# Block transposes by four SBUF-to-SBUF copies, in a two-layer decoder trunk on one Trainium2 core

## The chip, the core and the metric

The kernel runs on one NeuronCore of a Trainium2 chip: TensorE (PE, with its weight loads PEld), VectorE (DVE), ScalarE (ACT), GpSimd (POOL) and SyncE (SP), each with its own instruction queue, and 16 DMA engines that all queues share. SBUF and PSUM are on the core, HBM outside it. The metric is the device time of one execution in microseconds. Before the change it is 1225.33 us, the median of three runs (1224.45 to 1226.32).

## The reference

Two layers; each is a half-step feed-forward, a mixer of three branches, and a second half-step feed-forward. x is 256 tokens by 1024 channels, all in float32.

```python
for l in range(DEPTH):                                   # DEPTH = 2
    h = rms_norm(x, ffn1_norm_pre[l])
    x = x + 0.5 * rms_norm(swiglu(h, ffn1_w_in[l], ffn1_w_out[l]), ffn1_norm_post[l])
    h = rms_norm(x, mix_norm_pre[l])
    y = token_mixer(h, mem, cos, sin, mem_norm[l], w_mix_in[l], ...)
    x = x + rms_norm(y, mix_norm_post[l])
    h = rms_norm(x, ffn2_norm_pre[l])
    x = x + 0.5 * rms_norm(swiglu(h, ffn2_w_in[l], ffn2_w_out[l]), ffn2_norm_post[l])

# swiglu: a, b = split(h @ w_in); (silu(a) * b) @ w_out          D_FF = 2816
# token_mixer: one projection of h gives everything; then
#   short convolution; sparse attention (compressed, selected, window), 8 heads of 64;
#   cross-attention into 256 memory tokens, 4 heads of 128, keys and values = rms_norm(mem) @ w_mem_kv
#   merged = sum of sigmoid(gate_i) * (branch_i @ w_branch_i);  merged @ w_mix_out
```

## The kernel before

**Tiling.** The 256 tokens are two tiles of 128, called t = 0 and t = 1. Each is a stream (L1340) that runs through both layers; the two streams share each weight unit, and stream 0 may lead by up to three steps (LEAD). A step is six matmuls of 128x512 or as much. Every weight unit of 128x1024 words is loaded by SP into a buffer "raw" (four of them), and then split into a rounded part and a rest, "whi" by ACT (L309) and "wlo" by DVE (L310); each product is three matmuls (hi·hi, hi·lo, lo·hi). So ACT and DVE spend most of their time on these splits, which run ahead of TensorE as far as eight pairs of buffers let them.

**The order.** The program is written out step by step. `advance` (L349) counts steps; `later(n, fn)` puts work n steps on; `background` (L1231) lets the memory, compression and attention tasks each take a turn beside the streams. `prefetch` (L316) issues loads and splits some steps ahead of use. SP keeps the order as written; the order of the other engines is decided when the program is built. Each engine then runs its queue in that order, and an instruction that waits holds up everything behind it.

**The turn.** Activations have to change places: a tile with tokens on the partitions becomes one with channels on them. For the wide ones `turn` (L419) does this in two parts. DVE transposes 32x32 blocks inside the tile into "blocks" (L423). Then the 32x32 blocks themselves have to move between partition groups: one step later (AWAY) GpSimd issues four DMAs that write them to a scratch "there" in HBM (L428), and four steps after the start (BACK) one DMA that loads the scratch as "moved" (L440). That load waits on GpSimd for the landing of the four, and later DMAs queue behind it. At a fixed number of steps after the start, `turn_beside` (L448) splits "moved" into "turnhi" (ACT, L452) and "turnlo" (DVE, L453), which TensorE reads. The number is SPLIT = 12 in the feed-forward, ATT_T = 10 in attention, and KEYS = 18 for the memory's keys. There are 42 such turns: 24 in the feed-forwards (three per stream and feed-forward, the third 768 wide), 16 in attention and two for the memory's keys; the two of the memory in layer 0 come beside them.

**The memory.** `memory` (L688) normalizes the 256 memory tokens in two halves. In layer 0 each half is turned by way of its own scratch "mthere", with SPLIT steps to wait, and then scaled ("mf", L694). In layer 1 the halves are loaded again from mthere (RETURN = 6 steps). Then come two rounds of products with w_mem_kv, whose loads SP interleaves with the stream's own.

**Weights.** A turned tile has its rows in an order that the weights' rows have to match. For the five matrices in TURNED (L62) each unit is loaded by two DMAs, one for each half of the rows, to every second partition (L292).

**Prenorm.** At each sub-layer `postnorm` squares y on ACT ("junk", L463), updates x on DVE (L539); TensorE transposes x, and `prenorm` (L475) makes "hThi" on ACT (L491). TensorE cannot begin the next product before that.

Of the kernel before, what the change touches and what calls it, by code (L numbers as in the profile page):

```python
# [44 lines left out]
WARM = 5, 1, 2  # L45
KEYS, HALF, SECOND = 18, 5, 2
FRONT = True
# [6 lines left out]
NORM_B, NORM_C = 1, 1  # L54
AWAY, BACK, SPLIT, RETURN = 1, 4, 12, 6
DBUFS = 8
CONV, BS, CMP, ZC, QS_0, QS_1, QM, PC, YM = 4, 4, 6, 2, 2, 6, 2, 3, 1
ATT_A, ATT_B, ATT_C, ATT_D, ATT_T = 1, 3, 2, 6, 10
EARLY, RAMP, SCALES, STAGED, SETUP = 6, 10, 5, 8, 30
PACE, PACE_1, PACED = 9, 8, ("nsa", "memory")  # L60

TURNED = ("ffn1_w_out", "ffn2_w_out", "w_mix_out", "w_branch_conv", "w_branch_mem")  # L62
PRE = ("ffn1_norm_pre", "mix_norm_pre", "ffn2_norm_pre", "mem_norm")
# [59 lines left out]


def f32(ap):
    return ap.bitcast(F32)


def trunk_kernel(tc: tile.TileContext, a, out: bass.AP):
    with ExitStack() as ctx:  # L130
        def pool(name, bufs, **kw):
            return ctx.enter_context(tc.tile_pool(name=name, bufs=bufs, **kw))

        pools = dict(
            consts=pool("consts", 1), rawp=pool("rawp", RAWBUFS), wp=pool("wp", WBUFS), gp=pool("gp", GBUFS),
            gbp=pool("gbp", GAINS), tp=pool("tp", TBUFS), sp_pool=pool("sp", 2),
            dram=pool("dram", DBUFS, space=bass.MemoryType.DRAM),
            psa=pool("psa", ABUFS, space=bass.MemoryType.PSUM),
            pst=pool("pst", 8 - ABUFS, space=bass.MemoryType.PSUM))
        nothing = Nothing()  # L140
        plan = program(nothing, nothing, {k: nothing for k in pools}, nothing, nothing, None)
        with tc.manual_schedule(engines={mybir.EngineType.SP}):
            program(tc, tc.nc, pools, a, out, plan)


def program(tc, nc, pools, a, out, plan):
# [115 lines left out]
    def load(item, engines=None):  # L262
# [10 lines left out]
        for off, step, name, l, k0, nk, c0, n in parts:  # L273
# [144 lines left out]

    def turn(src, n, finish, wait, there=None):  # L419
        f = n // 4  # L420
        make = gtile if n > 512 else ttile
        blocks = make("blocks")
        nc.vector.transpose(blocks[:, :n], view(src, 0, [[32, 4], [P, n // P], [1, 32]]))  # L423
        there = dram.tile([P, 1024], F32, name="there", tag="d") if there is None else there

        def away():
            for q in range(4):
                nc.gpsimd.dma_start(there[:, q * f:(q + 1) * f].rearrange("(p j) f -> j p f", j=32),  # L428
                                    blocks[q * 32:(q + 1) * 32, :n].rearrange("j (p f) -> j p f", p=4))

        later(AWAY, away)
        back(there, n, finish, BACK, wait)

    def back(there, n, finish, start, wait):
        make = gtile if n > 512 else ttile
        moved = []

        def go():
            moved.append(make("moved"))
            nc.gpsimd.dma_start(moved[0][:, :n], there[:, :n])  # L440

        later(start, go)
        later(wait, lambda: finish(view(moved[0], 0, [[32, n // P], [n // 4, 4], [1, 32]])))

# [241 lines left out]
    mthere = [dram.tile([P, 1024], F32, name=f"mthere{i}", tag=f"m{i}", bufs=1) for i in range(2)]  # L686

    def memory(l):  # L688
        S = shared[l]
        H = []  # L690
        for mt in range(2):
# [9 lines left out]
            if l == 0:  # L701
# [3 lines left out]
                norm_scales(m, 0, mscale[mt])  # L705
                turn(m, 1024, gained, SPLIT, mthere[mt])
                yield SPLIT
            else:
                back(mthere[mt], 1024, gained, 0, RETURN)
                yield RETURN  # L710
# [12 lines left out]
        for mt in range(2):  # L723
            nc.scalar.activation(view(ks, mt * P, [[256, 4], [1, P]]), ps[mt].rearrange("p (h m) -> p h m", h=4),
                                 AF.Copy, scale=H[mt][1][0])

# [121 lines left out]

    def softmax_part(s3, dg, sums, place):
        n = s3.shape[1] if not dry else 1  # L850
# [3 lines left out]
        for i in range(n):  # L854
            dst, k = place(i)
            nc.scalar.activation(dst, s3[:, i], AF.Exp, bias=nm[:, i:i + 1], accum_out=sums[:, k:k + 1])

# [54 lines left out]
    def nsa_first(l, g):  # L912
# [4 lines left out]
        for u in range(2):  # L917
# [9 lines left out]
            def place(c):  # L927
                k = c % 2 * 4 + u * 2 + c // 2
                return p[:, k * P:(k + 1) * P], k

            s4 = s.rearrange("p (c k) -> p c k", c=4)
            softmax_part(s4, s4, sums, place)
        yield ATT_B
# [7 lines left out]
    def nsa_second(l, var, g):  # L941
# [5 lines left out]
        for u in range(2):  # L947
            s = bank("s")
            s3 = s.rearrange("p (i k) -> p i k", i=2)
            for i in range(2):  # L950
                for j in range(2):
# [3 lines left out]
            softmax_part(s3, s3[:, :, P:2 * P], sums,  # L955
                         lambda i: (view(p, (u * 2 + i) * P, [[512, 2], [1, P]]), u * 2 + i))
        yield ATT_B
# [159 lines left out]
    def mem_attention(l, u):  # L1117
# [5 lines left out]
        for t in range(2):  # L1123
# [11 lines left out]
            for i in range(2):  # L1135
                k = i * 2 + t
                nc.scalar.activation(view(p, k * P, [[512, 2], [1, P]]), s3[:, i], AF.Exp, bias=nm[:, i:i + 1],
                                     scale=scale, accum_out=sums[:, k:k + 1])
# [274 lines left out]
```

## Time and profile before

| | |
|---|---|
| median of three runs | 1225.33 us |
| profiled execution | 1228.28 us |
| its span, first to last instruction | 1226.6 us |
| mean granted TensorE clock | 0.994 |
| DMA packets | 281.63 MB, 230 GB/s in the mean |
| HBM read, written | 257.44 MB, 23.07 MB |
| longest shares of the chain that ended last | PE 70%, DMA 11%, DVE 8%, ACT 5% |

The profile is of one execution. Its tables count for each engine how long it was busy and, for each stretch of idle time, which event ended it. A row of a timeline has the start and the length in us, the engine, the line, what is written from what, and in brackets the idle time before it and what ended that. "PEclk" or the granted clock is the share of TensorE's full rate that it was given. A busy TensorE counts as busy at a low clock too, so both have to be read.

### The profile page before, as it was taken

Reading aid. Unit: us, or ns where it says so; the run is one execution under the profiler, and the core shown is the slowest. Engines: PE = TensorE matmul, PEld = TensorE weight load, DVE = VectorE, ACT = ScalarE, POOL = GpSimd, SP = SyncE. Lnnn points to the kernel's source line nnn. Section 1 sums busy time; section 2 is a strip of 40 time slices with the busy share of each in tenths; the row PEclk is TensorE's granted clock in tenths of the full one; section 3 lists DMA queues with packets and bytes.
Section 4 is the critical chain, followed back from the end, with each engine's and each line's share of the span. In section 5 each row is a group of like instructions: output and inputs, shape, how many; then the busy total and the mean of one; then the engine's idle time right before and its main releaser. Section 6 shows DMA issues by size and latency. Waiting matters only on the chain.

```text
span 1226.6 us, 16793 instructions
## 1 busy us (share of the span) xinstructions
PE 1192.9 (97%) x5776; PEld 1035.9 (84%) x5776; DVE 904.0 (74%) x1157; ACT 721.5 (59%) x1139; POOL 193.0 (16%) x383
## 2 busy tenths in 40 slices
PE   8999998999999999999999999999999989999997
PEld 6888877888888888888878888888878878888886
DVE  7867567798998776676576776578899866767753
ACT  6655345887876564554454554569878645645542
POOL 5011311311121010111011011013022200110110
PEclk9999998999999999999999999999999999999999
DMA  7888857677588757787757788858668866677772
GB/s 259 274 252 269 285 180 253 204 247 217 179 267 257 227 167 228 257 277 227 229 183 229 255 257 268 259 155 246 208 189 249 261 215 204 184 231 253 257 243 83
DMA packets 134293, 281.63 MB, mean 230 GB/s; under 512 B 13536, under 2 KB 32640, under 8 KB 134208
## 3 DMA queue, kind: packets, MB, share of 16 engines
q1 hardware_dynamic: 118752, 234.59, 60.9%
q0 software_dynamic: 15136, 45.44, 11.6%
q8 instruction: 45, 0.74, 0.2%
q10 hardware_dynamic: 320, 0.53, 0.1%
q14 instruction: 40, 0.33, 0.1%
HBM read 257.44 MB, written 23.07 MB: 229 GB/s over the span
## 4 chain that ended last, share of the span: by engine, by line
PE 70%; DMA 11%; DVE 8%; ACT 5%; issue 4%; POOL 2%; DVEq 0%; POOLq 0%; SPq 0%; ACTq 0%
PE acc L382 32%; PE acc L372 5%; PE acc L370 5%; PE acc L371 5%; PE y L372 5%; PE y L371 5%; PE y L370 5%; DMA moved<-there 3%; DVE wlo L310 3%; DMA there<-blocks 3%; DMA moved<-mthere 1%; ACT whi L309 1%; PE pt L413 1%; PE br L370 1%; PE br L372 1%
## 5 line engine op out<-in xcount | busy, mean ns | idle before, releaser
L310 DVE TENSOR_TENSOR wlo<-raw,whi 128x1024 fp32r<-128x1024 f32 (+2 forms) x441 | 530.8, 1212 | 185.6 <-ACT whi L309 181.7
L309 ACT CAST whi<-raw 128x1024 fp32r<-128x1024 f32 (+2 forms) x441 | 453.1, 1038 | 299.6 <-PE acc L382 155.1
L382 PE MATMUL acc<-whi,hThi 128*128 128x512 f32 x640 | 191.9, 381 | 3.2 <-ACT hThi L491 2.6
L382 PE MATMUL acc<-wlo,hThi 128*128 128x512 f32 x640 | 191.9, 380 | 0.1
L382 PE MATMUL acc<-whi,hTlo 128*128 128x512 f32 x640 | 191.6, 381 | 0.1
L370 PE MATMUL acc<-whi,hThi 128*128 128x512 f32 (+1 forms) x480 | 184.3, 384 | 3.6 <-ACT hThi L491 3.6
L371 PE MATMUL acc<-wlo,hThi 128*128 128x512 f32 (+1 forms) x480 | 180.5, 376 | 0.0
L372 PE MATMUL acc<-whi,hTlo 128*128 128x512 f32 (+1 forms) x480 | 180.1, 375 | 0.1
L428 POOL DMA_DIRECT2D there<-blocks x168 | 92.2, 555 | 451.0 <-DVE blocks L423 365.4
L382 PEld LDWEIGHTS acc<-whi,hThi 128*128 128x128 f32 x640 | 120.7, 189 | 21.6 <-ACT hThi L491 3.7
L382 PEld LDWEIGHTS acc<-whi,hTlo 128*128 128x128 f32 x640 | 121.1, 190 | 18.5 <-DVE hTlo L492 1.4
L382 PEld LDWEIGHTS acc<-wlo,hThi 128*128 128x128 f32 x640 | 121.3, 190 | 17.7 <-DVE wlo L310 0.5
L371 PE MATMUL y<-wlo,turnhi 128*128 128x512 f32 x352 | 133.4, 380 | 2.4 <-DVE wlo L310 2.4
L372 PE MATMUL y<-whi,turnlo 128*128 128x512 f32 x352 | 133.2, 379 | 0.0
L370 PE MATMUL y<-whi,turnhi 128*128 128x512 f32 x352 | 132.6, 379 | 0.0
L370 PEld LDWEIGHTS acc<-whi,hThi 128*128 128x128 f32 x480 | 91.4, 191 | 15.5 <-ACT hThi L491 4.8
L372 PEld LDWEIGHTS acc<-whi,hTlo 128*128 128x128 f32 x480 | 91.4, 190 | 12.6 <-DVE hTlo L492 0.3
L371 PEld LDWEIGHTS acc<-wlo,hThi 128*128 128x128 f32 x480 | 91.6, 191 | 10.3
L453 DVE TENSOR_TENSOR turnlo<-moved,turnhi 128x1024 fp32r<-128x1024 f32 (+1 forms) x42 | 49.2, 1170 | 54.1 <-ACT turnhi L452 54.0
L452 ACT CAST turnhi<-moved 128x1024 fp32r<-128x1024 f32 (+1 forms) x42 | 42.1, 1002 | 63.0 <-DMA moved<-there 54.9
L371 PEld LDWEIGHTS y<-wlo,turnhi 128*128 128x128 f32 x352 | 66.5, 189 | 12.1 <-DVE wlo L310 2.8
L370 PEld LDWEIGHTS y<-whi,turnhi 128*128 128x128 f32 x352 | 66.5, 189 | 9.4
(302 smaller groups left out, 1458.6 us busy)
## 6 DMA issues: line engine op xcount, KB each, us to landing
raw<-in_ffn_w_in_dram SPq DMA_DIRECT2D x159, 512.0 KB, 4.9
raw<-in_w_mix_in_dram SPq DMA_DIRECT2D x96, 512.0 KB, 4.8
raw<-in_ffn_w_out_dram SPq DMA_DIRECT2D x176, 256.0 KB, 4.3
there<-blocks POOLq DMA_DIRECT2D x136, 128.0 KB, 4.5
moved<-there POOLq DMA_DIRECT2D x34, 512.0 KB, 5.2
raw<-in_ffn_w_in_dram SPq DMA_DIRECT2D x33, 256.0 KB, 4.1
raw<-in_w_mem_kv_dram SPq DMA_DIRECT2D x16, 512.0 KB, 6.1
raw<-in_w_mix_out_dram SPq DMA_DIRECT2D x32, 256.0 KB, 3.5
```

The lines of the kernel that those rows point to most:

```text
L309: pinned(nc.scalar.copy(hi[:, c0:c1], raw[:, c0:c1]))
L310: pinned(nc.vector.tensor_sub(lo[:, c0:c1], raw[:, c0:c1], f32(hi[:, c0:c1])))
L370: nc.tensor.matmul(ps, lhsT=xh, rhs=wh, start=start, stop=False, skip_group_check=skip)
L371: nc.tensor.matmul(ps, lhsT=xh, rhs=wl, start=False, stop=False, skip_group_check=skip)
L372: nc.tensor.matmul(ps, lhsT=xl, rhs=wh, start=False, stop=stop, skip_group_check=skip)
L382: pinned(nc.tensor.matmul(p[:, :n], lhsT=hT[x2][:, k], rhs=moving(w, j * n, n), start=(k == 0 and i == 0), stop=(k == 7 and i == 2)))
L413: pinned(nc.tensor.transpose(pt[:, j * P:(j + 1) * P], src[:, c0 + j * P:c0 + (j + 1) * P], ident))
L428: nc.gpsimd.dma_start(there[:, q * f:(q + 1) * f].rearrange("(p j) f -> j p f", j=32), blocks[q * 32:(q + 1) * 32, :n].rearrange("j (p f) ...
L452: nc.scalar.copy(hv, mv)
L453: nc.vector.tensor_sub(lv, mv, f32(hv))
```

## The change

The scratch in HBM goes. The four DMAs write straight into "moved" in SBUF, one step after the transpose, and the load back is gone. Because the four DMAs now place partition 4j + p where the load had placed 32p + j, the order of what is turned changes with them:

- Softmax results are written in the new order: the Exp on ACT reads PSUM at a stride of four words and writes runs of 32 (`lanes_in`, `lanes_out`). The keys are copied in the same way.
- The weight rows follow: TURNED becomes RUNS, with runs of 16 rows for both w_out and of 64 for the other three matrices, and the unit is loaded by one DMA per 128 rows instead of two of 64 partitions.
- The memory's halves are copied to mthere after their use, for layer 1.
- The steps to wait fall: SPLIT 12 to 8, ATT_T 10 to 7, KEYS 18 to 13; BACK and the eight scratch buffers go.

```diff
-KEYS, HALF, SECOND = 18, 5, 2
+KEYS, HALF, SECOND = 13, 5, 2
-AWAY, BACK, SPLIT, RETURN = 1, 4, 12, 6
-DBUFS = 8
+AWAY, SPLIT, RETURN = 1, 8, 6
-ATT_A, ATT_B, ATT_C, ATT_D, ATT_T = 1, 3, 2, 6, 10
+ATT_A, ATT_B, ATT_C, ATT_D, ATT_T = 1, 3, 2, 6, 7
-TURNED = ("ffn1_w_out", "ffn2_w_out", "w_mix_out", "w_branch_conv", "w_branch_mem")
+RUNS = {"ffn1_w_out": 16, "ffn2_w_out": 16, "w_mix_out": 64, "w_branch_conv": 64, "w_branch_mem": 64}
+def lanes_in(ap, c, n=P):
+    return view(ap, c, [[P, n // P], [1, 4], [4, 32]])
+def lanes_out(ap, c, dims):
+    return view(ap, c, [list(d) for d in dims] + [[32, 4], [1, 32]])
...
-                if name in TURNED:
-                    for h in range(2):
-                        rows = src.rearrange("(k h i) n -> h i k n", h=2, i=64)[h]
-                        nc.sync.dma_start(view(raw[h:P:2], off, [[step, nk], [1, n]]), rows)
+                if name in RUNS:
+                    rows = src.rearrange("(k v u) n -> k u v n", k=nk, u=RUNS[name])
+                    for k in range(nk):
+                        nc.sync.dma_start(raw[:, off + k * step:off + k * step + n], rows[k])
...
-    def turn(src, n, finish, wait, there=None):
+    def turn(src, n, finish, wait, order=(32, 1)):
...
-        nc.vector.transpose(blocks[:, :n], view(src, 0, [[32, 4], [P, n // P], [1, 32]]))
-        there = dram.tile([P, 1024], F32, name="there", tag="d") if there is None else there
+        nc.vector.transpose(blocks[:, :n], view(src, 0, [[order[0], 4], [P, n // P], [order[1], 32]]))
+        moved = []
         def away():
+            moved.append(make("moved"))
             for q in range(4):
-                nc.gpsimd.dma_start(there[:, q * f:(q + 1) * f].rearrange("(p j) f -> j p f", j=32),
+                nc.gpsimd.dma_start(moved[0][:, q * f:(q + 1) * f],
                                     blocks[q * 32:(q + 1) * 32, :n].rearrange("j (p f) -> j p f", p=4))
         later(AWAY, away)
-        back(there, n, finish, BACK, wait)
-    def back(there, n, finish, start, wait):
...
-            nc.gpsimd.dma_start(moved[0][:, :n], there[:, :n])
-        later(start, go)
+        later(wait, lambda: finish(turned_view(moved[0], n)))
...
+    def keep(mt, gained):
+        def finish(mv):
+            gained(mv)
...
+            nc.gpsimd.dma_start(mthere[mt], whole)
+    def back(mt, gained):
+        moved = gtile("moved")
+        nc.gpsimd.dma_start(moved, mthere[mt])
+        later(RETURN, lambda: gained(turned_view(moved, 1024)))
...
-            nc.scalar.activation(dst, s3[:, i], AF.Exp, bias=nm[:, i:i + 1], accum_out=sums[:, k:k + 1])
+            nc.scalar.activation(dst, lanes_in(s3[:, i], 0, width), AF.Exp, bias=nm[:, i:i + 1],
+                                 accum_out=sums[:, k:k + 1])
```

The built order moves at places where the diff shows nothing. On ACT at the first mixer's prenorm of stream 0 in layer 0, up to the hThi that TensorE needs ("ks" are the memory's keys, "vm" its values; 560 wide splits are of the mixer's second group of columns), the rows before are

```order
L463 ACTIVATE junk,ss_1829<-y_1231 128x512
L463 ACTIVATE junk,ss_1829<-y_1232 128x512
L309 CAST whi<-raw 128x1024
L724 ACTIVATE ks<-acc,mscale_127 128x4x128
L309 CAST whi<-raw 128x1024
L724 ACTIVATE ks<-acc,mscale_128 128x4x128
L309 CAST whi<-raw 128x1024 x5
L491 CAST hThi<-hf 128x512 x2
```

and of the change

```order
L414 ACTIVATE vm<-acc,mscale_127 128x512
L414 ACTIVATE vm<-acc,mscale_128 128x512
L316 CAST whi<-raw 128x1024
L316 CAST whi<-raw 128x560
L464 ACTIVATE junk,ss_1859<-y_1218 128x512
L464 ACTIVATE junk,ss_1859<-y_1219 128x512
L464 ACTIVATE junk,ss_1900<-x_88 128x512
L492 CAST hThi<-hf 128x512 x2
```

Seven splits and both copies of the keys stood between junk and hThi; now they, and the values too, stand ahead of junk. On ACT at the boundary of layer 0 and layer 1, stream 0 again, the rows before are

```order
L309 CAST whi<-raw 128x1024 x13
L463 ACTIVATE junk,ss_5859<-y_5417 128x512
L309 CAST whi<-raw 128x1024
L463 ACTIVATE junk,ss_5859<-y_5418 128x512
L309 CAST whi<-raw 128x1024 x4
L491 CAST hThi<-hf 128x512 x2
```

and of the change

```order
L316 CAST whi<-raw 128x1024 x17
L464 ACTIVATE junk,ss_5766<-y_5345 128x512
L464 ACTIVATE junk,ss_5766<-y_5346 128x512
L464 ACTIVATE junk,ss_5807<-x_88 128x512
L492 CAST hThi<-hf 128x512 x2
```

The five splits between the first junk and hThi have moved ahead of junk. On DVE at the last attention turn of layer 1 ("p" are the probabilities, "yf" the sums over branches' heads, "gth" and "merged" the gated merge), from the transpose to its turnlo, the rows before are

```order
L423 STREAM_TRANSPOSE blocks<-p 128x1024
L893 TENSOR_TENSOR yf<-o,yf 64x512
L310 TENSOR_TENSOR wlo<-raw,whi 128x1024
L893 TENSOR_TENSOR yf<-o,yf 64x512
L453 TENSOR_TENSOR turnlo<-moved,turnhi 128x1024
L310 TENSOR_TENSOR wlo<-raw,whi 128x1024 x2
L1326 SCALAR_TENSOR_TENSOR gth<-gth,br 128x512
L1327 TENSOR_TENSOR merged_8715<-merged_8715,gth 128x512
L310 TENSOR_TENSOR wlo<-raw,whi 128x1024 x2
L453 TENSOR_TENSOR turnlo<-moved,turnhi 128x1024
```

where the first turnlo belongs to the turn before, and of the change

```order
L430 STREAM_TRANSPOSE blocks<-p 128x1024
L317 TENSOR_TENSOR wlo<-raw,whi 128x1024 x3
L1340 SCALAR_TENSOR_TENSOR gth<-gth,br 128x512
L454 TENSOR_TENSOR turnlo<-moved,turnhi 128x1024
```

turnlo stands three splits behind its blocks instead of five, and the previous turn's turnlo is already done.

More of the change, by code (lines that the diff above doesn't have):

```diff
@@ L136, in trunk_kernel @@
             gbp=pool("gbp", GAINS), tp=pool("tp", TBUFS), sp_pool=pool("sp", 2),
-            dram=pool("dram", DBUFS, space=bass.MemoryType.DRAM),
+            dram=pool("dram", 1, space=bass.MemoryType.DRAM),
             psa=pool("psa", ABUFS, space=bass.MemoryType.PSUM),
@@ L422, in turn, with turned_view @@
         blocks = make("blocks")
-        nc.vector.transpose(blocks[:, :n], view(src, 0, [[32, 4], [P, n // P], [1, 32]]))
-        there = dram.tile([P, 1024], F32, name="there", tag="d") if there is None else there
+        nc.vector.transpose(blocks[:, :n], view(src, 0, [[order[0], 4], [P, n // P], [order[1], 32]]))
+        moved = []
         def away():
+            moved.append(make("moved"))
             for q in range(4):
-                nc.gpsimd.dma_start(there[:, q * f:(q + 1) * f].rearrange("(p j) f -> j p f", j=32),
+                nc.gpsimd.dma_start(moved[0][:, q * f:(q + 1) * f],
                                     blocks[q * 32:(q + 1) * 32, :n].rearrange("j (p f) -> j p f", p=4))
         later(AWAY, away)
-        back(there, n, finish, BACK, wait)
-    def back(there, n, finish, start, wait):
[L435 to L440, printed above, removed]
-        later(start, go)
-        later(wait, lambda: finish(view(moved[0], 0, [[32, n // P], [n // 4, 4], [1, 32]])))
+        later(wait, lambda: finish(turned_view(moved[0], n)))
+        return moved
+    def turned_view(moved, n):
+        return view(moved, 0, [[32, n // P], [n // 4, 4], [1, 32]])
     def quarters(ap, c):
@@ L686, in program @@
     mthere = [dram.tile([P, 1024], F32, name=f"mthere{i}", tag=f"m{i}", bufs=1) for i in range(2)]
+    def keep(mt, gained):
+        def finish(mv):
+            gained(mv)
+            whole = bass.AP(tensor=mv.tensor, offset=mv.offset, ap=[list(mv.ap[0]), [1, 1024]]) if not dry else mv
+            nc.gpsimd.dma_start(mthere[mt], whole)
+        return finish
+    def back(mt, gained):
+        moved = gtile("moved")
+        nc.gpsimd.dma_start(moved, mthere[mt])
+        later(RETURN, lambda: gained(turned_view(moved, 1024)))
     def memory(l):
@@ L705, in memory @@
                 norm_scales(m, 0, mscale[mt])
-                turn(m, 1024, gained, SPLIT, mthere[mt])
+                turn(m, 1024, keep(mt, gained), SPLIT, (1, 4))
                 yield SPLIT
             else:
-                back(mthere[mt], 1024, gained, 0, RETURN)
+                back(mt, gained)
                 yield RETURN
@@ L723, in memory @@
         for mt in range(2):
-            nc.scalar.activation(view(ks, mt * P, [[256, 4], [1, P]]), ps[mt].rearrange("p (h m) -> p h m", h=4),
-                                 AF.Copy, scale=H[mt][1][0])
+            nc.scalar.activation(lanes_out(ks, mt * P, [[256, 4]]), lanes_in(ps[mt], 0, 512), AF.Copy,
+                                 scale=H[mt][1][0])
         def keys(hi, lo):
@@ L847, in recip_gate, with softmax_part @@
         return r
-    def softmax_part(s3, dg, sums, place):
+    def softmax_part(s3, dg, sums, place, width):
         n = s3.shape[1] if not dry else 1
@@ L928, in place @@
                 k = c % 2 * 4 + u * 2 + c // 2
-                return p[:, k * P:(k + 1) * P], k
+                return lanes_out(p, k * P, [[0, 1]]), k
             s4 = s.rearrange("p (c k) -> p c k", c=4)
-            softmax_part(s4, s4, sums, place)
+            softmax_part(s4, s4, sums, place, P)
         yield ATT_B
@@ L955, in nsa_second @@
             softmax_part(s3, s3[:, :, P:2 * P], sums,
-                         lambda i: (view(p, (u * 2 + i) * P, [[512, 2], [1, P]]), u * 2 + i))
+                         lambda i: (lanes_out(p, (u * 2 + i) * P, [[512, 2]]), u * 2 + i), 2 * P)
         yield ATT_B
@@ L1136, in mem_attention @@
                 k = i * 2 + t
-                nc.scalar.activation(view(p, k * P, [[512, 2], [1, P]]), s3[:, i], AF.Exp, bias=nm[:, i:i + 1],
+                nc.scalar.activation(lanes_out(p, k * P, [[512, 2]]), lanes_in(s3[:, i], 0, 2 * P), AF.Exp, bias=nm[:, i:i + 1],
                                      scale=scale, accum_out=sums[:, k:k + 1])
```

## The prediction

> **What bounds the kernel now.** I read the page first, then a table of stretches, then the waits, then the timeline around each place where TensorE stood. The page's first section gives the frame:
>
> ```profile
> PE 1192.9 (97%) x5776; PEld 1035.9 (84%) x5776; DVE 904.0 (74%) x1157; ACT 721.5 (59%) x1139; POOL 193.0 (16%) x383
> ```
>
> TensorE is busy 97% of a 1226.6 us span, and the change leaves all 5776 matmuls in place. So the time can only move in the 33.7 us in which TensorE stands, and in stretches where its granted clock is low. The table of stretches says where those are (columns: length, busy time of PE, PEld, DVE, ACT and POOL with their counts, granted clock, DMA share, GB/s):
>
> ```profile
> 20.00:130.00 110.00, 110.00 (x511) 95.77 (x511) 83.41 (x101) 61.59 (x68) 20.45 (x37) 1.00 0.84 270
> 130.00:180.00 50.00, 47.58 (x221) 41.20 (x220) 26.34 (x26) 20.62 (x27) 11.43 (x24) 1.00 0.66 223
> 180.00:225.00 45.00, 40.92 (x185) 34.70 (x184) 32.49 (x42) 26.06 (x45) 7.81 (x15) 0.92 0.72 227
> 250.00:320.00 70.00, 66.35 (x373) 58.10 (x372) 63.14 (x128) 56.91 (x122) 9.69 (x19) 1.00 0.67 207
> 390.00:410.00 20.00, 19.44 (x92) 16.23 (x91) 17.17 (x19) 11.86 (x14) 0.00 (x0) 1.00 0.72 223
> 410.00:600.00 190.00, 189.65 (x892) 165.42 (x891) 129.84 (x135) 96.72 (x114) 21.88 (x40) 1.00 0.74 233
> 600.00:630.00 30.00, 28.03 (x129) 23.72 (x128) 20.74 (x30) 16.49 (x29) 4.33 (x10) 0.94 0.51 155
> 740.00:770.00 30.00, 29.08 (x134) 24.84 (x133) 19.60 (x18) 14.57 (x15) 4.35 (x8) 1.00 0.80 257
> 800.00:830.00 30.00, 29.31 (x153) 25.09 (x152) 21.60 (x32) 19.89 (x45) 4.67 (x12) 1.00 0.52 148
> 850.00:920.00 70.00, 66.82 (x378) 58.38 (x377) 63.02 (x127) 57.08 (x123) 10.36 (x19) 1.00 0.66 206
> 955.00:975.00 20.00, 18.03 (x87) 15.39 (x86) 16.81 (x25) 13.85 (x27) 2.74 (x5) 1.00 0.76 243
> 995.00:1015.00 20.00, 16.34 (x68) 12.97 (x67) 15.95 (x18) 10.68 (x13) 0.00 (x0) 0.91 0.52 160
> ```
>
> A feed-forward stretch (20 to 130) is solid: 511 matmuls in 110 us, 0.215 us each, so one step of the program (six matmuls) is 1.3 us. For the others I count standing time (length minus PE busy) plus clock time (1 minus the granted clock, times the length): A 130–180: 2.4. B 180–225: 4.1 + 3.6 = 7.7. Early attention, 250–320 and 850–920: 3.65 + 3.2. I 390–410: 0.6. C 600–630: 2.0 + 1.8 = 3.8. G 740–770: 0.9. D 955–975: 2.0. E 995–1015: 3.7 + 1.8 = 5.5. That is 29.8 us, and it is the whole stake. The clock is low only in B, C and E, each time behind a stop of 1.9 to 3.3 us (rows below). [...]
>
> **The change part by part.** *The return trip.* A turn was four pieces to HBM, a wait, and one load back; now the four pieces land where they are read.
>
> ```profile
> raw<-in_ffn_w_in_dram SPq DMA_DIRECT2D x159, 512.0 KB, 4.9
> raw<-in_ffn_w_out_dram SPq DMA_DIRECT2D x176, 256.0 KB, 4.3
> there<-blocks POOLq DMA_DIRECT2D x136, 128.0 KB, 4.5
> moved<-there POOLq DMA_DIRECT2D x34, 512.0 KB, 5.2
> out_dram<-x SPq DMA_DIRECT2D x4, 256.0 KB, 2.0
> ```
>
> What goes is the 5.2 us load, its issue, and GpSimd's wait for the pieces. No row shows an SBUF-to-SBUF piece. It has the read side of "there<-blocks" (4.5 us) and the write side of "moved<-there"; I take 4.5, the nearer in size; the ends are 2.0, the shortest landing of a large transfer in the list, and 9.0, nearly both legs one after the other. [...]
>
> *E, the last attention turn of layer 1*, is the plainest term:
>
> ```profile
> 977.83 1.25 DVE L423 STREAM_TRANSPOSE blocks<-p 128x1024 f32<-128x1024 f32 x1 [0.70 <-ACT p L961]
> 979.37 2.19 POOL L428 DMA_DIRECT2D there<-blocks  x4 [3.64 <-DVE blocks L423]
> 986.85 0.56 POOL L440 DMA_DIRECT2D moved<-there  x1 [5.30 <-DMA there<-blocks]
> 994.74 1.04 ACT L452 CAST turnhi<-moved 128x1024 fp32r<-128x1024 f32 x1 [7.66 <-DMA moved<-there]
> 1005.05 0.48 PE L370 MATMUL br<-whi,ynsa 128*128 128x512 f32 x1 [3.16 <-ACT ynsa L901]
> ```
>
> The blocks are ready at 979.1, and turnhi starts at 994.74. With the pieces in place it could start at about 986.4, just before the old return was issued, 8.3 us sooner. The place of this br among TensorE's matmuls stays: as much work lies between it and the last score matmul as before. TensorE's wait is 3.16 us and its clock term 1.8, so half of the 8.3 would do. What is late next is DVE: its rows under the change put turnlo three splits and a merge behind blocks where it was five splits, a merge, two sums and another turnlo, so ACT, and DVE behind it, will still stand some 3 us there in place of 7.66. I take E from 5.5 to 0.6, the loss at the same place in layer 0 (I): minus 4.9, ends minus 5.5 and minus 1.5. I itself: minus 0.5. D is DVE late behind an earlier turn of the same chain:
>
> ```profile
> 958.27 1.23 DVE L453 TENSOR_TENSOR turnlo<-moved,turnhi 128x1024 fp32r<-128x1024 f32 x1 [2.69 <-ACT turnhi L452]
> PE br L370 <- DVE gth L1326: 2.0, 1, 2.0
> ```
>
> That turn's return was issued late, behind another instruction on GpSimd; without it half of D goes, minus 1.0, ends 0 and minus 2.0.
>
> *B, the first mixer's prenorm:*
>
> ```profile
> 203.33 1.04 ACT L309 CAST whi<-raw 128x1024 fp32r<-128x1024 f32 x1 [3.09 <-DMA raw<-in_w_mem_kv_dram]
> 204.28 1.13 ACT L491 CAST hThi<-hf 128x512 fp32r<-128x512 f32 x2
> 204.95 0.79 PE L370 MATMUL acc<-whi,hThi 128*128 128x512 f32 x1 [3.32 <-ACT hThi L491]
> ```
>
> A weight split waits 3.09 us for a load of w_mem_kv, and hThi, for which TensorE stands, is queued behind it on ACT. SPLIT drops by 4 for both halves of the memory, so the memory's products, and SP's eight w_mem_kv loads with them, come eight steps (10.4 us) sooner, into the end of the feed-forward, where no prenorm waits. The order shows it: no split is left between junk and hThi. Layer 1 already has its memory there, and its prenorm (800–830) loses 0.7. So 7.7 becomes 0.7: minus 7.0, ends minus 7.7 and 0.
>
> *C, the layer boundary:*
>
> ```profile
> 614.74 1.04 ACT L309 CAST whi<-raw 128x1024 fp32r<-128x1024 f32 x1 [0.47 <-DMA raw<-in_ffn_w_in_dram]
> 615.69 1.13 ACT L491 CAST hThi<-hf 128x512 fp32r<-128x512 f32 x2
> 616.35 0.48 PE L382 MATMUL acc<-whi,hThi 128*128 128x512 f32 x1 [1.94 <-ACT hThi L491]
> ```
>
> Five splits stood between junk and hThi; in the new order none does, as at the other boundaries, whose long stretch 410–600 loses 0.35 in all. Why the splits moved is not in the diff, and the splits still want their loads, so I take two thirds: minus 2.4, ends minus 3.8 and 0.
>
> *A and G, the memory's turns.*
>
> ```profile
> 171.56 0.58 POOL L440 DMA_DIRECT2D moved<-mthere  x1 [6.16 <-DMA mthere<-blocks]
> 175.23 1.23 DVE L694 TENSOR_TENSOR mf<-moved,gT 128x1024 f32<-128x1024 f32 x1 [9.15 <-DMA moved<-mthere]
> ```
>
> DVE stands 9.15 us, and the weights behind it come 2.4 us late. The data now come about 4.2 us sooner (171.0 for 175.2), but the use is put four steps, 5.2 us, sooner. Those nearly cancel; that the catching-up is shorter and the first half's wait is folded into another's stands on either side. I take half, minus 1.2, ends minus 2.4 and plus 3. G waits for loads from mthere that were issued behind a turn's return wait on GpSimd; with no such wait it goes by 0.6, ends 0 and minus 0.9. The new copy "mthere<-moved" adds two DMAs behind each half's landing on GpSimd; what is queued behind them is the next half's pieces, eight steps later: nothing.
>
> *Shorter distances.* SPLIT 12 to 8 and ATT_T 10 to 7 put turnhi and turnlo 5.2 and 3.9 us nearer to their blocks, while the chain shortens by about 5.8 (5.2 and the issue). Where the chain was late it is now less late; where it had room, the room stays about equal. In the feed-forward pairs the second turn will stop ACT some 2 to 5 us. The cover is the lead of the splits:
>
> ```profile
> ACT whi L309 <- PE acc L382: 155.1, 125, 1.7
> ACT turnhi L452 <- DMA moved<-there: 54.9, 18, 7.7
> 137.57 0.83 ACT L452 CAST turnhi<-moved 128x768 fp32r<-128x768 f32 x1 [5.50 <-DMA moved<-there]
> ```
>
> ACT waits 155 us in total for TensorE to free weight buffers, so the splits run ahead; the stop of 5.50 us at 137.57 left TensorE no wait of its own. Cost nothing there; without the cover, a stop would cost its length. In attention DVE is 63 of 70 us busy, so I add 2.5 us over both layers (ends 0 and 6) and credit 1.0 to the early gaps (ends 0 and minus 2).
>
> *Weights and softmax.* w_out loads become one DMA of 512 KB instead of two of 256: 4.9 for 4.3 us by the rows above, under the same lead: nothing. Exp now reads PSUM at a stride of four words and writes runs of 32:
>
> ```profile
> L856 ACT ACTIVATE p<-s,nm 128x256 f32<-128x256 f32 x32 | 14.8, 468 | 5.5 <-DVE nm L853 5.4
> L813 ACT ACTIVATE qs<-acc,rs 128x512 f32<-128x512 f32 x4 | 2.7, 684 | 0.1
> L1103 ACT ACTIVATE qms<-acc,rs 128x512 f32<-128x512 f32 x4 | 2.7, 684 | 0.0
> ```
>
> The qs row reads PSUM at a stride of two and takes 684 ns like the plain qms row, so I take nothing. The other end is a doubling of the Exp rows' own 468 ns, 15 us of ACT in stretches with 13 us free of 70: perhaps 4 us.
>
> **The sum.** E 4.9, I 0.5, D 1.0, B 7.0, C 2.4, A 1.2, G 0.6, early attention 1.0 are 18.6 off; shorter distances put 2.5 on: minus 16.1. The profiled execution took 1228.28 us (span 1226.6 and 1.7 around it), so 1212.2 against itself; it lies 2.95 above the median of 1225.33, and against that the forecast is **1209 us**.
>
> **Rivals.** *R1, slower: the pieces land late.* If an SBUF-to-SBUF piece takes 9 us under load, a turn lasts as long as before, but its use is 3 or 4 steps nearer. Sixteen attention turns would each stop ACT and DVE some 4.5 us longer, 72 us in all; DVE has 7 us free in 70 by the rows above, 28 in the 280 us in which these turns stand, so some 40 us of lateness fall on the splits' lead, of which I let half through: 1225 plus 20, less B's 7: 1238. It decides from about 8 us; for it, the rings are 0.7 to 0.9 busy; against it, both legs land in about 5. *R2: B and C stay*, because the splits, now ahead of junk, wait for their loads there: 1209 + 9.4 = 1218. Against it, layer 1's row. *R3, no change: the gain is given back* by turnhi stopping ACT in front of the splits in twelve feed-forward turns at 1.3 us each: 1225. Against it, the 5.50 us stop that cost nothing.
>
> **How the numbers follow.** Forecast (1202 to 1214) 0.66; R2 0.15; R3 0.09; R1 0.10. The range 1201 to 1222 holds the first two and the sum's own ends (early attention, D and A at their best: minus 5; Exp, A and the distances at their worst: plus 10). A measurement of this kernel can tell about 0.2%, 2.5 us, from no change. Faster 0.83, same 0.08, slower 0.09.
>
> **What would show it.** "moved<-blocks" landing in about 4.5 us; no wait of TensorE for hThi over 1 us in the first mixer's prenorm and at the layer boundary; no stretch of low clock but the start and end; "br<-ynsa" without a wait. Wrong it would be with landings over 8 us, with ACT's waits for DMA at turnhi well above 54.9 us and TensorE waiting for wlo, or with Exp rows above 468 ns.

## The result and the profile after

The change is slower: 1242.3 us (median of four runs, 1240.88 to 1245.22) against 1225.82 us for the kernel before (four runs, 1224.45 to 1227.03). The ratio is 1.0138, with an interval of 1.0116 to 1.0160. The forecast was 1209, the range 1201 to 1222.

The page of the change begins with:

```profile
PE 1194.1 (96%) x5776; PEld 1037.5 (84%) x5776; DVE 906.6 (73%) x1157; ACT 721.6 (58%) x1141; POOL 172.3 (14%) x341
```

Of a span of 1240.1 us TensorE now stands 46.0 instead of 33.7. The table of stretches, at the same places in the program as in the prediction (after the first loss everything stands 8 to 15 us later; columns as there), says where:

```profile
20.00:130.00 110.00, 110.00 (x511) 95.57 (x510) 81.88 (x98) 59.90 (x66) 18.08 (x33) 1.00 0.81 238
130.00:180.00 50.00, 39.81 (x171) 33.32 (x170) 26.61 (x25) 18.01 (x25) 12.94 (x23) 0.93 0.78 198
180.00:235.00 55.00, 50.00 (x227) 42.96 (x227) 37.04 (x46) 30.17 (x48) 6.57 (x13) 0.94 0.69 199
262.00:333.00 71.00, 67.94 (x386) 59.25 (x385) 65.56 (x131) 58.24 (x130) 10.21 (x19) 1.00 0.62 191
375.00:385.00 10.00, 8.03 (x39) 6.73 (x38) 9.57 (x13) 7.58 (x16) 2.17 (x4) 1.00 0.71 230
402.00:424.00 22.00, 22.00 (x105) 19.10 (x105) 18.90 (x22) 13.08 (x15) 0.00 (x0) 1.00 0.74 221
610.00:640.00 30.00, 25.85 (x115) 22.19 (x114) 20.89 (x27) 16.80 (x27) 3.17 (x6) 0.89 0.69 213
860.00:933.00 73.00, 68.70 (x395) 60.13 (x393) 66.04 (x130) 59.90 (x127) 10.77 (x18) 1.00 0.64 197
968.00:988.00 20.00, 17.44 (x86) 14.93 (x85) 18.31 (x27) 13.36 (x27) 4.33 (x8) 1.00 0.74 218
1008.00:1030.00 22.00, 22.00 (x106) 19.07 (x105) 19.03 (x21) 12.30 (x15) 0.00 (x0) 1.00 0.75 225
```

Counted as in the prediction (standing plus clock), place by place; the last column is the kernel v1 below, which keeps the copies but mends the two faults found here:

| place | before | the change | forecast difference | measured difference | v1 |
|---|---|---|---|---|---|
| A, memory's start | 2.4 | 10.2 + 3.5 | -1.2 | +11.3 | 0 |
| B, first mixer's prenorm | 7.7 | 5.0 + 3.3 | -7.0 | +0.6 | 0 |
| early attention, both layers | 6.8 | 7.4 | +1.5 | +0.5 | 9.7 |
| D, and its twin in layer 0 | 2.0 | 2.6 + 2.0 | -1.0 | +2.6 | 2.5 |
| C, layer boundary | 3.8 | 4.15 + 3.3 | -2.4 | +3.7 | 0.25 |
| G, memory of layer 1 | 0.9 | 0 | -0.6 | -0.9 | 0 |
| E and I, last attention turns | 6.1 | 0 | -5.4 | -6.1 | 0 |

(Early attention takes the forecast's minus 1.0 and plus 2.5 together.) Most of the loss is at A, the rest at C and D; B only changed its cause; E, I and G came as forecast. One more loss stands behind the last matmul, where the forecast looked at nothing: from there to the end it takes 9.29 us in the change and 6.39 before. In the trace's records GpSimd's DRAIN at the end of the program lasts 7.54 us (1231.79 to 1239.33) where it lasted 2.48 (1221.14 to 1223.62), and the other engines, done 2.9 us earlier, wait for it. Both lengths are the same in every run below, the long one in all that have the copies, the short one in e2 and e3, which have not; so the copies bring these 2.9 us with them, and why is not shown. With them the places add up to 14.6 us; the two profiled executions differ by 13.6.

The list of DMAs (KB each, median us from issue to landing) shows what had not been priced:

```profile
raw<-in_ffn_w_in_dram SPq DMA_DIRECT2D x159, 512.0 KB, 4.9
raw<-in_ffn_w_out_dram SPq DMA_DIRECT2D x88, 512.0 KB, 6.8
moved<-blocks POOLq DMA_DIRECT2D x144, 128.0 KB, 4.4
moved<-blocks POOLq DMA_DIRECT2D x32, 96.0 KB, 7.9
```

The pieces of 128 KB land in 4.4 us, as assumed (4.5). But the load of w_out takes 6.8 us, where a load of w_in of the same size takes 4.9; and the smaller pieces of 96 KB, which move while w_out is loaded, take 7.9. The queues' part of the page, of before and of the change, tells what the packets cost (packets, MB, share of 16 engines' span):

```profile
q1 hardware_dynamic: 118752, 234.59, 60.9%
```

```profile
q1 hardware_dynamic: 117088, 234.58, 65.3%
```

The same bytes take 65.3% of 1240.1 us in place of 60.9% of 1226.6, 63 us more on each of 16 engines. If w_out's 88 x 128 packets are the cause, that is some 90 ns for each. The trace's packet records agree: SP's packets of 4 KB in w_out's stretches take 280 ns in the mean where they took 197, and their median, used from here on, goes from 159 to 282 ns. So by the medians a unit of w_out, 128 packets on 16 engines, keeps each engine busy for 2.26 us of the two steps (2.6 us) for which it lasts, where it was 1.27 (an estimate, eight packets to each engine).

The waits (engine and line, waited for, us in total, times, longest) show what it does to ACT:

```profile
ACT whi L316 <- PE acc L389: 109.9, 100, 1.9
ACT turnhi L453 <- DMA moved<-blocks: 106.4, 28, 7.7
ACT whi L316 <- DMA raw<-in_ffn_w_out_dram: 59.8, 45, 3.8
```

Before, the first two were 155.1 and 54.9, and the third

```profile
ACT whi L309 <- DMA raw<-in_ffn_w_out_dram: 14.6, 9, 2.5
```

ACT waits less for TensorE, so the splits no longer run ahead as far; it waits twice as long for the pieces, and four times as long for w_out. TensorE's four longest waits in the timeline are

```profile
158.90 0.79 PE L378 MATMUL y<-wlo,turnhi 128*128 128x512 f32 x1 [6.53 <-DVE wlo L317]
219.43 0.90 PE L420 MATMUL pt<-ident,x 128*128 128x128 f32 x3 [4.05 <-DVE x L540]
628.92 1.08 PE L420 MATMUL pt<-ident,x 128*128 128x128 f32 x4 [4.15 <-DVE x L540]
983.81 0.48 PE L377 MATMUL br<-whi,ymemh 128*128 128x512 f32 x1 [2.56 <-DVE gth L1340]
```

The first is A; the second and third are B and C, where TensorE no longer waits for hThi but, a few instructions earlier, for x; the fourth is D. What precedes A is a stop of ACT, 46 us earlier (timeline of ACT in the change):

```profile
104.89 1.05 ACT L316 CAST whi<-raw 128x1024 fp32r<-128x1024 f32 x1 [0.60 <-PE acc L389]
112.77 1.04 ACT L453 CAST turnhi<-moved 128x1024 fp32r<-128x1024 f32 x1 [6.83 <-DMA moved<-blocks]
113.72 1.99 ACT L316 CAST whi<-raw 128x1024 fp32r<-128x1024 f32 x2
```

I define the lead of a split as the time from the end of its wlo to the first matmul that reads it; the times given are those at which the wlo starts. In the change the lead is 11.1 us up to this stop, 4.7 behind it, back at 9.3 by 131 us, and 0.06 us at 145.6, behind two more stops (7.69 and 2.98 us) for the narrow turns. TensorE stands for 2.3 us there (145.66 and 146.92), and now little is left between a wait on DVE and TensorE. DVE has one:

```profile
156.48 1.23 DVE L707 TENSOR_TENSOR mf<-moved,gT 128x1024 f32<-128x1024 f32 x1 [8.48 <-DMA moved<-blocks]
157.62 2.35 DVE L317 TENSOR_TENSOR wlo<-raw,whi 128x1024 fp32r<-128x1024 f32 x2
```

mf waits 8.48 us for the memory's pieces, and the wlo behind it is the one that TensorE awaits at 158.90. At the layer boundary it is the same: the lead is 0.06 us at 592, and between 1.6 and 4.5 us from there up to 617, because each split finds its w_out load late; x is then late by what the splits in front of junk are late. (At B the waits table puts the longest of these waits, 4.00 us before the split at 209.15, down to TensorE, which freed a buffer in the same moment. The load that this split reads landed at 209.05, and the splits beside it start 0.08 to 0.10 us behind their loads too; so here as well the load was waited for.)

### The profile page after: what moved, and what is told of

It reads as the page before. It is cut to its first block, busy times and chain, and to the rows that moved or that the text cites. A ratio compares the mean times of both kernels' runs of the same rounds, so it can differ in the third digit from the quotient of the medians.

```text
span 1240.1 us, 16547 instructions
## 1 busy us (share of the span) xinstructions
PE 1194.1 (96%) x5776; PEld 1037.5 (84%) x5776; DVE 906.6 (73%) x1157; ACT 721.6 (58%) x1141; POOL 172.3 (14%) x341
## 3 DMA queue, kind: packets, MB, share of 16 engines
q1 hardware_dynamic: 117088, 234.58, 65.3%
## 5 line engine op out<-in xcount | busy, mean ns | idle before, releaser
L436 POOL DMA_DIRECT2D moved<-blocks x176 | 96.0, 565 | 664.9 <-DVE blocks L430 299.6
L378 PE MATMUL y<-wlo,turnhi 128*128 128x512 f32 x352 | 136.6, 388 | 7.8 <-DVE wlo L317 7.8
L377 PE MATMUL y<-whi,turnhi 128*128 128x512 f32 x352 | 135.3, 384 | 1.5 <-ACT whi L316 1.5
L379 PE MATMUL y<-whi,turnlo 128*128 128x512 f32 x352 | 136.1, 387 | 0.0
L453 ACT CAST turnhi<-moved 128x1024 fp32r<-128x1024 f32 (+1 forms) x42 | 42.2, 1004 | 107.7 <-DMA moved<-blocks 106.4
L378 PEld LDWEIGHTS acc<-wlo,hThi 128*128 128x128 f32 x480 | 90.9, 189 | 10.2
```

The source lines that it names most:

```text
L377: nc.tensor.matmul(ps, lhsT=xh, rhs=wh, start=start, stop=False, skip_group_check=skip)
L378: nc.tensor.matmul(ps, lhsT=xh, rhs=wl, start=False, stop=False, skip_group_check=skip)
L379: nc.tensor.matmul(ps, lhsT=xl, rhs=wh, start=False, stop=stop, skip_group_check=skip)
L436: nc.gpsimd.dma_start(moved[0][:, q * f:(q + 1) * f], blocks[q * 32:(q + 1) * 32, :n].rearrange("j (p f) -> j p f", p=4))
L453: nc.scalar.copy(hv, mv)
```

## Experiments

In the runs of these experiments the kernel before had medians of 1222.3 to 1224.6 us, and single runs from 1215 to 1236; so each kernel is judged by its ratio to the runs of before on the same chip. An interval behind a ratio is one of 95%. The first theories were R (the new order of rows makes the loads of w_out slow), W (the shorter waits stop ACT and DVE too early) and M (one DMA of 512 KB is slower than two of 256 KB).

**Which rows a load reads.** Two kernels are the change with another order of rows for w_out (the rows then stand in the wrong partitions, so only the time of these two tells something):

```diff
-RUNS = {"ffn1_w_out": 16, "ffn2_w_out": 16,
+RUNS = {"ffn1_w_out": 128, "ffn2_w_out": 128,    # e1_rows_as_they_lie
+RUNS = {"ffn1_w_out": 32, "ffn2_w_out": 32,      # o1_runs_of_32
```

> The change, but both w_out are loaded with 128 rows in the order in which they lie in HBM (a run of 128 in place of runs of 16; one DMA of 512 KB as in the change). The rows then stand in the wrong partitions, so the product with w_out is not the reference's; every instruction of the engines is that of the change, in the same order. Theory R (row order): in the change a packet of 4 KB of w_out took 282 ns in the median where it took 159 before, and the load 6.8 us; here packets fall back to about 159 ns, the load to about 4.9 us, ACT's wait for w_out from 59.8 us to below 20, the loss at 130 to 180 us from 13.6 us to 3 to 5 us, and the time from 1242 to 1226, range 1220 to 1232. Theory W (the waits are too short, SPLIT 8 and ATT_T 7) and theory M (one DMA of 512 KB in place of two of 256 KB): no change, 1242, within 3.

> The change with w_out loaded in runs of 32 rows (the product with w_out is not the reference's; all engines' orders are those of the change). [...] If there is a bound between 16 and 64, packets are at 159 ns and the time at 1222, or at 280 ns and 1242.

The ratios are 0.9980 (0.9949 to 1.0010) and 0.9978 (0.9945 to 1.0010). In both, packets are back at a median of 159 ns; the DMA list of the second says

```profile
raw<-in_ffn_w_out_dram SPq DMA_DIRECT2D x88, 512.0 KB, 4.9
moved<-blocks POOLq DMA_DIRECT2D x32, 96.0 KB, 4.2
```

So the order of rows alone takes the whole loss away, with every instruction of the engines in its place. In the packets there is a bound between runs of 16 and runs of 32, and no slope: 282 ns, then 159 for 32, 64 and 128. The pieces of 96 KB land in 4.2 us again: they had been slow because of w_out, not because SBUF was their source and end.

Two kernels are the kernel before, with the same change of rows or with one DMA alone:

```diff
-                        rows = src.rearrange("(k h i) n -> h i k n", h=2, i=64)[h]
+                        rows = src.rearrange("(w h u) n -> h u w n", h=2, u=16)[h]        # e2, w_out only
...
-                    for h in range(2): ...
+                    nc.sync.dma_start(raw[:, off:off + n], src.rearrange("(v u) n -> u v n", u=64))   # e3, w_out only
```

> The kernel before, with two DMAs of 64 partitions as there, but each reads the rows of w_out in the order of the change (runs of 16). The rows then stand in the wrong partitions, so the product with w_out is not the reference's; the engines' instructions and their order are those of before. Theory R: packets of w_out at 250 to 290 ns, and the time from 1225 to 1236, range 1230 to 1246. Theories W and M: 1225, within 3, because neither the waits nor the number of DMAs change.

> The kernel before, with w_out loaded by one DMA of 128 partitions in runs of 64: the same rows in the same partitions as before. The built order of the engines differs a little from before, since the number of DMAs has a part in it. Theory M: w_out loads at 6 to 7 us, time 1234 or more. Theory R: packets stay at 159 ns, loads at 4.5 to 5 us, time 1225, within 5 (the built order may give or take some).

e2 has a ratio of 1.0054 (1.0027 to 1.0081), e3 of 0.9994 (0.9969 to 1.0019). One DMA of 512 KB costs nothing (4.9 us to landing, packets at 159 ns). Runs of 16 are slower with the old way of moving blocks too, packets at a median of 226 ns, but they cost 0.5%, two fifths of what the change lost and less than theory R had expected (250 to 290 ns, 1230 us or more; the median was 1228.66). The loss needs something else beside them.

**Which wait is too short.** Five kernels give steps back to the change:

```diff
-AWAY, SPLIT, RETURN = 1, 8, 6
+AWAY, SPLIT, RETURN = 1, 12, 6                     # e4, s1, v5
-KEYS, HALF, SECOND = 13, 5, 2
+KEYS, HALF, SECOND = 18, 5, 2                      # e4, s2
-ATT_A, ATT_B, ATT_C, ATT_D, ATT_T = 1, 3, 2, 6, 7
+ATT_A, ATT_B, ATT_C, ATT_D, ATT_T = 1, 3, 2, 6, 10 # e4, s2
...
-                turn(m, 1024, keep(mt, gained), SPLIT, (1, 4))
-                yield SPLIT
+                turn(m, 1024, keep(mt, gained), 12, (1, 4))    # v4: 12; v5: 8
+                yield 12
```

> The change with the steps to wait of before: SPLIT 12, ATT_T 10, KEYS 18. Theory W: ACT's wait for the pieces falls from 106 us to below 50, and the time to 1225 to 1230. Theory R: the loads of w_out stay at 6.8 us, and the time stays above 1236 (the longer waits hide late pieces, but not late weights).

> The change with SPLIT alone back at 12 (ATT_T 7 and KEYS 13 stay). Theory S (the shorter SPLIT does the harm: the feed-forward's turnhi stops ACT, the splits lose their lead and cannot win it back against loads of 6.6 us, and the memory's first half waits for its pieces in front of the weights): 1223, range 1218 to 1228, without the loss at 130 to 180 us beyond 5 us and without the waits for x at the prenorms. Rival A (the attention's shorter ATT_T and KEYS do it): above 1235.

> The change with ATT_T back at 10 and KEYS at 18 (SPLIT stays 8). Theory S: still 1238 or more, with the losses at 130 to 180 us and at the layer boundary as in the change. Rival A: 1223, range 1218 to 1230.

> The change with 12 steps for the feed-forward's turns only; the memory's halves keep 8. SP's and TensorE's orders are those of the change. Theory L (the feed-forward's turnhi and turnlo stop ACT and DVE 8 steps behind the blocks, the splits' lead is used up, and slow w_out loads do not let it grow again): the waits for x at the prenorms go, some 8 us and more with the lead at the memory's start: 1229, range 1224 to 1234. Theory Mw (the memory's halves, 8 steps behind their transpose, in front of the weights on DVE): 1238 or more.

> The change with 12 steps for the memory's halves only; the feed-forward's turns keep 8. Theory L: 1236, range 1231 to 1243, with the waits for x at the layer boundary still there. Theory Mw: 1226, range 1222 to 1230.

| kernel | feed-forward | memory | attention, keys | ratio to before |
|---|---|---|---|---|
| the change | 8 | 8 | 7, 13 | 1.0138 (1.0116 to 1.0160) |
| e4 | 12 | 12 | 10, 18 | 1.0012 (0.9985 to 1.0038) |
| s1 | 12 | 12 | 7, 13 | 0.9983 (0.9965 to 1.0000) |
| v5 | 12 | 8 | 7, 13 | 0.9988 (0.9958 to 1.0018) |
| v4 | 8 | 12 | 7, 13 | 1.0163 (1.0111 to 1.0215) |
| s2 | 8 | 8 | 10, 18 | 1.0157 (1.0130 to 1.0184) |

Among the waits the feed-forward's decides alone; those of the memory, the attention and the keys do not matter to the loss. e4 went against theory R, which had expected over 1236: with 12 steps the slow loads are nearly free. v5 did better than theory L had expected (1221.5 for 1229), although the memory kept its 8 steps. In v5, whose orders on SP and TensorE are those of the change, ACT's timeline at the place of the first stop reads

```profile
110.16 1.05 ACT L316 CAST whi<-raw 128x1024 fp32r<-128x1024 f32 x1 [1.54 <-PE acc L389]
111.67 0.69 ACT L567 ACTIVATE th<-acc,rs 128x512 f32<-128x512 f32 x1 [0.46 <-PE acc L389]
112.75 1.05 ACT L316 CAST whi<-raw 128x1024 fp32r<-128x1024 f32 x1 [0.39 <-PE acc L389]
113.70 1.04 ACT L453 CAST turnhi<-moved 128x1024 fp32r<-128x1024 f32 x1
```

turnhi starts 0.9 us later than in the change, and waits for nothing; in place of 6.83 us of standing ACT did three splits. The lead is 11.1 us behind this place, and its lowest value at the layer boundary is 4.9 us, for 0.06. ACT's waits for w_out are still there (42.7 us in 26 times), and TensorE feels little of them: its longest wait for x is 1.8 us. In v4 the stops and the lead of 0.06 us at 147 are back, and with them 8.2 us of TensorE's waits for wlo:

```profile
PE y L378 <- DVE wlo L317: 8.2, 3, 3.8
PE pt L420 <- DVE x L540: 4.6, 4, 3.6
```

**A load in two halves**, with the change's mapping of rows:

```diff
-                    for k in range(nk):
-                        nc.sync.dma_start(raw[:, off + k * step:off + k * step + n], rows[k])
+                    for h in range(2):                                             # w_out only
+                        nc.sync.dma_start(raw[h * 64:(h + 1) * 64, off:off + n], rows[0][h * 8:(h + 1) * 8])
```

> The change with w_out loaded by two DMAs of 64 adjacent partitions each, in the same mapping of rows to partitions (eight of the 16 runs in each DMA). If packets are slow because all 16 DMA engines read rows next to each other in the same moment, this halves the crowd: packets between 170 and 240 ns, loads at 5 to 6 us, time 1226 to 1236. If the stride of 16 rows within one engine is what counts, packets stay at 280 ns, and the time at 1238 or more (the built order differs a little, since the number of DMAs has a part in it).

The time was far outside both cases: the ratio is 1.0707 (1.0663 to 1.0750). The table of stretches has, in the second feed-forward of layer 0,

```profile
580.00:625.00 45.00, 36.02 (x156) 28.74 (x155) 22.66 (x25) 15.01 (x19) 4.34 (x8) 0.99 0.54 134
```

TensorE stands 9 of 45 us, ACT waits 171 us in all for w_out, and yet the DMA engines are busy only 54% at 134 GB/s. In the packet records SP's queue has, from 585 to 620 us, eight packets open for 62% of the time, and more than nine for 5%; in the change, from 565 to 600, 14 to 18 for 68%. So about half as many packets are open at a time. The outermost dimension of a w_out load is 16 in the change and 8 in each DMA here; the two halves also write 64 adjacent partitions each, where the loads of before write every second one. No run separates the two. The question of crowding, for which the kernel was made, stays open: the 4 KB packets have medians of 280 ns in one stretch (780 to 820) and of 165 in another (1235 to 1270), and which rows the engines read at the same moment stands in no record.

**Both remedies.** With runs of 64 for w_out the result has to be written in another order, by the gate's last operation on DVE. f1, the change with this alone, reads at a stride of four words and writes runs of 32, in one instruction for each 128 columns; v1 and v2 write at a stride of 32:

```diff
-            nc.vector.scalar_tensor_tensor(both[:, c0:c0 + n], th[:, :n], r2_half, pb[:, :n], ...)
+            for c in range(0, n, P):       # f1: out [[32, 4], [1, 32]], in [[1, 4], [4, 32]]
+                nc.vector.scalar_tensor_tensor(view(both, c0 + c, [[1, 32], [32, 4]]), view(th, c, [[4, 32], [1, 4]]),
+                                               r2_half, view(pb, c, [[4, 32], [1, 4]]), ...)
```

v3 is e1 with SPLIT 12; v1 has SPLIT 12; v2 has all three waits of before.

> [...] Theory R: w_out packets 159 ns, loads 4.9 us, ACT's wait for w_out below 20 us, as in the kernel with rows as they lie; time 1221, range 1216 to 1228. Against it stands the price on DVE: the transpose with a stride of four words took 2964 ns for 1236; at the same factor 2.4 the last operation of the gate costs 1.0 us more for each 512 columns, some 40 us of DVE in all, in stretches in which DVE is 0.76 busy, and the time is 1224 to 1232.

> The change with SPLIT 12 and w_out loaded in the order in which its rows lie (the product with w_out is not the reference's). If slow rows and short waits only harm together, either remedy alone takes all that is to be had, and both give 1221, within 3. If each also costs something by itself, both give 1213 to 1217.

> SPLIT 12 and w_out in runs of 64, with the gate's last operation reading in order and writing at a stride of 32 words (one instruction for each 128 columns). With the reads at a stride of four words such an instruction took 540 ns. If it is the read that costs, it takes some 250 ns here, and the time is that of rows as they lie with SPLIT 12, plus at most 2. If the write costs as much, 500 ns or more, and the time is 4 to 5 us above it, as it was in the pair with SPLIT 8 (1226 for 1222).

> The gate written at a stride of 32 words, w_out in runs of 64, and all three waits of before (SPLIT 12, ATT_T 10, KEYS 18). If the copies themselves bring the gain, 1217, range 1214 to 1220. If the shorter ATT_T and KEYS bring it, 1221 to 1224, with the wait of br for ynsa back in layer 0 or 1.

| | w_out in runs of 16 | fast rows |
|---|---|---|
| SPLIT 8 | 1.0138 (the change) | 0.9980 (e1); 1.0019, 0.9992 to 1.0045 (f1) |
| SPLIT 12 | 0.9983 (s1) | 0.9945, 0.9917 to 0.9973 (v3); 0.9949, 0.9922 to 0.9976 (v1) |
| SPLIT 12, ATT_T 10, KEYS 18 | 1.0012 (e4) | 0.9963, 0.9940 to 0.9985 (v2) |

From v3, slow rows alone cost 0.4% (s1), the short wait alone 0.35% (e1), and both together 1.9%: the sum would be 0.75%. Some 14 us, 1.2%, come of the two together. That each also harms a little by itself, as v3's second case has it (1213 to 1217 us; it took 1216.17), is near the noise: the interval of v3 overlaps those of s1 and e1. v1 computes what the kernel before does, and beats it: 1216.92 us for 1222.84 on the same chip. v2's interval covers v1's value, so the gain comes with the copies and the new order; that the shorter waits of attention add to it is not shown. The table of stretches for v1 has, at the memory's start, the first mixer's prenorm and the layer boundary,

```profile
130.00:180.00 50.00, 50.00 (x234) 43.78 (x233) 35.74 (x33) 25.37 (x32) 11.27 (x22) 1.00 0.77 259
180.00:225.00 45.00, 45.00 (x236) 39.98 (x235) 34.74 (x47) 31.80 (x67) 9.86 (x18) 1.00 0.70 210
600.00:630.00 30.00, 29.75 (x145) 25.36 (x144) 25.07 (x36) 17.90 (x30) 5.33 (x10) 1.00 0.59 181
```

and the gate's last operation on DVE stands in the groups of f1, of v1 and of the change (count, busy us, mean ns) as

```profile
L573 DVE SCALAR_TENSOR_TENSOR wide<-th,rs,acc 128x128 f32<-128x128 f32 x176 | 83.3, 540 | 3.3
```

```profile
L573 DVE SCALAR_TENSOR_TENSOR wide<-th,rs,acc 128x128 f32<-128x128 f32 x176 | 54.9, 430 | 3.3
```

```profile
L572 DVE SCALAR_TENSOR_TENSOR wide<-th,rs,acc 128x512 f32<-128x512 f32 x40 | 29.9, 748 | 3.2
```

The expectation on v1 had named 250 ns or over 500, and it is 430. What counts is the busy time, since such instructions overlap (176 times 540 ns would be 95 us): 83.3 us with strided reads, 54.9 with strided writes, and 33.7 in the change (3.8 of them for 256 columns). A part of the 21 us more in v1 may come of four instructions in place of one; no run separates that from the writes. 50 us more of DVE cost f1 some 0.4% against e1 (its 1226.25 us lies in both ranges of its expectation); 21 us more cost v1 nothing against v3.

## Why the prediction was wrong, step by step

- **The weights: "4.9 for 4.3 us by the rows above, under the same lead: nothing".** This is the first step that failed. The 4.9 us came from a load of the same size that reads its rows as they lie. No row of before shows a load that reads rows 16 apart, and that should have been bounded from both sides, not read from a neighbour. It measured 6.8 us, and ACT's wait for w_out went from 14.6 to 59.8 us. With faster rows the loss is gone (e1, o1).
- **Shorter distances: "Cost nothing there; without the cover, a stop would cost its length".** This is the second. The cover, the lead of the splits, was real, but it was taken as if it were there afresh for each stop. It is a store: the stops take from it, and it fills again only as fast as loads come beyond TensorE's need. ACT's wait for the pieces rose from 54.9 to 106.4 us, while slow loads took the filling away. The slow loads make the stops longer, too: with the same 8 steps and fast rows (e1) the wait is 72.8 us. In e1 the lead falls to 7.5 us at the layer boundary and is back at 10.4 two splits later; in the change it falls to 0.06 and has not come above 4.5 by 617 us. Either alone is borne; both are not. The prediction's own sign of being wrong, ACT's waits at turnhi well above 54.9 us and TensorE waiting for wlo, came true. That they multiply is shown by the table of the two remedies, and that the feed-forward's wait is the one by v5 and v4.
- **A, minus 1.2, ends minus 2.4 and plus 3.** It measured plus 11.3. The lead was used up before it, and the memory's pieces landed 12.9 us behind the end of their transpose (156.40 for 143.48). I had missed three things: the transpose reads at a stride of four words now and takes 2964 ns for 1236; two of the pieces were issued 4.7 and 5.4 us behind its end, behind the scales that GpSimd works out; and these two took 6.5 and 7.5 us to land, beside loads of w_out, where the median of their size is 4.4. The memory's wait does not decide by itself: in v5 the memory's wait is as short, and A is 2.1.
- **B and C, minus 7.0 and minus 2.4.** The waits for hThi went, as the order had shown, and waits for x took their place. That is rival R2, by its mechanism ("the splits, now ahead of junk, wait for their loads there"), which I had given 0.15, with nothing against it but layer 1's row. In v1, with a lead, both places are empty (0 and 0.25 us): the reading of the order was right, and its condition failed.
- **E and I, minus 4.9 and minus 0.5; G, minus 0.6.** Right, and slightly too small: the three places stand for nothing now.
- **D, minus 1.0.** Wrong sign: the wait of br for gth is 2.6 us, and has a twin of 2.0 in layer 0. v1 has them too (1.5 and 1.0). Why they stay is open.
- **The end.** No term stood for it; GpSimd's longer DRAIN costs 2.9 us there.
- **The pieces and Exp.** Right: 4.4 us for 4.5 assumed, and Exp takes 475 and 368 ns for 468 and 369.
- **R1, slower, 1238.** It came near in time and not in mechanism: pieces of 128 KB took 4.4 us in the median, the 96 KB ones 7.9, and these were late because of w_out's rows; the attention's turns did not bring the loss, and giving back their steps (s2) did not help.
- **The size of the stake.** v1 has the terms of the forecast at A, B, C, E and I, and its profiled execution, 1214.84 us, is near the 1212.2 that the sum gave against the profile of before; but in part that is luck: the places that it mended gave some 4 us more than forecast, while D, early attention (2.9 us more than before, where the forecast had 1.5) and the end took more than that back. Its median is only 0.5% below before. The stake was read from one execution, at 1228.28 us, and the later medians of before are 1222.3 to 1224.6; so a part of the standing time counted on may belong to that execution alone, and how much is not shown.

## What to carry to other kernels

A lead is a store with a rate of filling: before a wait is shortened behind which prefetched work is queued, look at how much of the lead the waits take, one after another, and whether the loads run faster than they are used. A change of layout can also change the order in which a load reads its rows; a load in a new order needs a price of its own, and the times of its packets give it. Time behind the last matmul belongs to the sum as well. Two costs that are each hidden under the same cover have to be tried together.

## What the runs showed of the hardware

- Loads of 128 rows of 4 KB in runs of 16, so that neighbouring partitions get rows 16 apart: packets at a median of 282 ns (the change); in runs of 32 (o1), of 64 (v1) and as the rows lie (e1): 159 ns. In two loads of 64 rows each, to every second partition, runs of 16 gave 226 ns (e2). Why there is a bound between 16 and 32 is not shown.
- DVE reading SBUF at a stride of four words: 2964 ns for 1236 in a transpose of 128x1024, 2.4 times as long; why is not shown. ACT's Exp reading PSUM at the same stride cost next to nothing (475 ns for 468).
- The clock: before, a stop of 1.94 us (616.35) was followed by 3.4 us at half the clock (0.50 granted from 618 to 620), and one of 2.42 us (177.65) by none (1.00 from 175 to 188), which the prediction's reading of the rows passed over; in the change one of 2.56 us (983.81) was followed by none either (1.00 from 980 to 990). In these traces the length of a stop alone does not decide it.
- GpSimd's DRAIN at the end of the program: 2.48 us in the three kernels that go through HBM, 7.54 us in the thirteen that copy within SBUF. Why is not shown.
